# Repeating the rows of 16-wide diagonal blocks over partitions: lane shuffles on VectorE in place of selection matmuls and copies

## The chip, the cores and the metric

The kernel runs on one core of a Trainium2 chip. The metric is the device time of one execution in microseconds (us), the median over several runs. The engines are named as in the profile: PE (TensorE matmul), PEld (TensorE weight load), DVE (VectorE), ACT (ScalarE), POOL (GpSimd) and SP (SyncE). SP issues most of the loads from memory.

## The reference

The program is two layers of a hybrid backbone: 256 latent tokens and 256 context tokens of width 1024. Each layer has an input projection, three token mixers side by side (Hyena, gated DeltaNet, latent attention), a gated merge with an output projection, and a mixture of 16 experts. The second layer does not update the context. The part that matters here is the gated DeltaNet, with four heads, two directions and chunks of 64 tokens:

```python
m = jnp.where(strict, jnp.einsum('nbhid,nbhjd->nbhij', kb, kc) * gamma, 0.0)
t_inv = lax.linalg.triangular_solve(eye + m, jnp.broadcast_to(eye, m.shape), left_side=True, lower=True, unit_diagonal=True)
u = t_inv @ (vc * bc[..., None])
w = t_inv @ (kb * jnp.exp(gc)[..., None])
a_intra = jnp.einsum('nbhid,nbhjd->nbhij', qc, kc) * gamma
def step(s, xs):
    u_n, w_n, a_n, qd_n, kd_n, ge_n = xs
    v_new = u_n - w_n @ s
    o_n = qd_n @ s + a_n @ v_new
    s = s * ge_n[..., None, None] + jnp.swapaxes(kd_n, -1, -2) @ v_new
    return s, o_n
```

Every 64-wide chunk needs the inverse of a unit triangular matrix. The kernel builds it from the inverses of 16-wide diagonal blocks.

## The kernel before

The whole program is one stream of instructions per engine, and the order on each engine is fixed when the program is built. A planner keeps a virtual clock per engine (`Plan.enter`, line 254). The large projections are *items*: lists of matmuls with their weight loads and a step behind them. The mixers are *streams*, Python generators that give control back at each `yield`. After each piece of an item, `Trunk.tick` (line 490) takes the stream step that `best` (line 483) names: one whose inputs should be ready by PE's virtual clock, and only while at least 3 of the PSUM banks and some pages are free. `prep_ahead` (line 516) starts preparation of later items, and stops when VectorE's virtual clock runs far ahead of PE's. `fill` (500) and `drain` (510) run stream steps when an item must wait for data or for a stream. So the costs that `enter` charges, and the places of the `yield`s, decide which item matmuls stand on PE between the steps of a mixer.

All intermediate arrays lie in pages of 4 KB per partition, `NPAGE` of them (line 40, 45 pages), handed out by an `Arena` (line 145). Weights go to pages too, so a load waits on SP until its page is free. In the trace the page of an operand is only "pg", a PSUM bank "bank", and all instructions recorded through a helper carry line L210; so the trace is read by tiles and shapes.

The delta rule runs per layer in two streams, `gdn_pair` (line 930) for head pair 0 ("gdn0") and head pair 1 ("gdn1"). Each pair calls `gdn_system` (lines 1044 to 1200) twice, for the context tokens (base 2) and for the latent tokens (base 0), the second as a stream of its own, "gdnsys0" or "gdnsys1", started while the pair goes on. That makes 8 systems in the program. `gdn_scan` (line 1202) then runs the recurrence, the pair norms and transposes its output, and the items of the delta rule's branch come after.

One system holds 8 matrices of 128x128 (two directions, two chunk pairs, two heads). Its steps:

- E is the decay, G the key products, N the negated strict part of the system. `C` takes N's 16-wide diagonal blocks, packed as [128 partitions, 8 matrices, 16], plus the identity (lines 1084 to 1094). These are DVE operations.
- For the substitution each partition needs, of its own 16-row block, every row k. The 16 rows are repeated over their partitions: `rsel` holds 16 selection matrices of 128x128, and for each k one matmul of R[:, k, :] with the 128 elements of C (X16 from element 256) gives row k of each block on all 16 partitions (lines 1103 to 1108). Four k fill one PSUM bank, ACT copies the bank to the pages `B`, and `Bv` (line 1116) is a view of those by k. The trace shows 2 records to a matmul: 32 per system.
- The substitution (lines 1117 to 1126) goes from j = 14 down to 0 on DVE: one or two products and a reduce each, over X, P and Bv, with a `yield` after j = 10, 7, 5, 3 and 1.
- T, the inverses in block-diagonal form, is transposed on PE (weights "cst", the identity), merged from 16 to 32 to 64 by matmul groups of four 128x128 and then 64x64, with ACT and DVE operations between them that PE's next group waits for, and so is a chain over several engines.

The selection matrices come from the columns 2048 to 4095 of a constant table in memory. `late_setup` (line 2433) allocates `rsel` (8 KB per partition, 1 MB) and loads it on ACT's queue once (lines 2441 and 2442).

The items of the merge are here called gate items: of the gates of a branch, 128x512 matmuls in layer 0 and 128x256 in layer 1. `layer` (line 2293) sets their order after the mixers' items. In layer 0 a stream "filters" (started by an item hook) prepares the Hyena filters of layer 1 with 128x512 matmuls.

## Time and profile before

| | us |
|---|---|
| runs, lowest, median, highest | 2143.21, 2144.14, 2147.01 |
| the profiled execution | 2145.01 |
| its span, first to last instruction | 2143.0 |
| PE busy | 1919.7 (90%) |
| DVE busy | 1274.2 (59%) |
| ACT busy | 869.3 (41%) |
| POOL busy | 340.8 (16%) |
| mean granted TensorE clock | 0.945 |

The profiled execution is 2.0 us longer than its span and 0.87 us above the median. Busy shares are means over stages. Layer 0's mixers run from about 100 to 760 us, the experts of layer 0 to about 1200, layer 1's mixers to about 1760, its experts and the final norm to the end. In a window row the figures behind the length are the busy times of PE, PEld, DVE, ACT and POOL with the number of instructions, then the granted clock, the DMA share and the transfer rate.

### The profile page before, as it was taken

The numbers are of one execution on the slowest core, as the hardware profiler recorded it, in microseconds if no ns is written. First come the engines' busy times: TensorE is split into PE (matmuls) and PEld (weight loads), VectorE is DVE, ScalarE is ACT, GpSimd is POOL, SyncE is SP. The second block draws the span as 40 slices with busy tenths as digits, with TensorE's granted clock in tenths as the row PEclk, the third lists the DMA queues.
The fourth block names the chain that finished last, engine by engine and source line by source line (L and its number), as shares of the span: only waits on it lengthen the run. The fifth ranks groups of instructions, "written<-read, shape, count | busy, mean of one in ns | idle before, by whom it ended". The sixth has DMA issues, their size and how long they took to land. (4 is left out here: it accounts for less than half of the span.)

```text
span 2143.0 us, 31289 instructions
## 1 busy us (share of the span) xinstructions
PE 1919.7 (90%) x11901; PEld 1434.8 (67%) x11902; DVE 1274.2 (59%) x2487; ACT 869.3 (41%) x1443; POOL 340.8 (16%) x318
## 2 busy tenths in 40 slices
PE   4999999999999898799999399988999987899993
PEld 1777887877778586688777277887787976433330
DVE  3656657555466646899888676666766666311113
ACT  3442334444433323388777444433454442010101
POOL 1211122000133003411100201221011212110002
PEclk9899999999999799899999799999999998899996
DMA  9735223312533156799997567422223448899971
GB/s 330 223 96 182 60 58 94 89 50 79 158 99 85 58 180 223 256 361 382 377 358 248 173 205 234 126 55 75 79 60 109 119 138 331 294 383 389 382 269 67
DMA packets 295751, 403.62 MB, mean 188 GB/s; under 512 B 43956, under 2 KB 185786, under 8 KB 295464
## 3 DMA queue, kind: packets, MB, share of 16 engines
q1 hardware_dynamic: 271512, 360.38, 50.4%
q10 hardware_dynamic: 13040, 21.33, 2.8%
q0 software_dynamic: 11040, 19.81, 2.7%
q8 instruction: 96, 1.57, 0.3%
q14 instruction: 63, 0.52, 0.1%
HBM read 394.56 MB, written 23.20 MB: 195 GB/s over the span
## 5 line engine op out<-in xcount | busy, mean ns | idle before, releaser
L210 PE MATMUL bank<-pg,pg 128*128 128x512 f32 (+5 forms) x9958 | 1701.7, 407 | 44.3 <-DVE pg L210 23.4
L210 PEld LDWEIGHTS bank<-pg,pg 128*128 128x128 f32 (+3 forms) x9958 | 1247.5, 172 | 445.9 <-issue 204.4
L210 DVE TENSOR_TENSOR pg<-pg,pg 128x1024 fp32r<-128x1024 f32 (+10 forms) x696 | 606.1, 901 | 217.7 <-ACT pg L210 206.9
L210 ACT CAST pg<-pg 128x1024 fp32r<-128x1024 f32 (+3 forms) x460 | 428.9, 965 | 260.9 <-DVE pg L210 167.4
L210 ACT COPY pg<-bank 128x512 f32<-128x512 f32 (+4 forms) x382 | 185.0, 506 | 368.2 <-PE bank L210 335.3
L210 PE MATMUL bank<-cst,pg 128*128 128x128 f32 (+3 forms) x935 | 145.0, 292 | 90.7 <-DVE pg L210 51.9
L210 PEld LDWEIGHTS bank<-cst,pg 128*128 128x128 f32 (+1 forms) x935 | 118.8, 160 | 149.5 <-issue 54.1
L210 POOL TENSOR_TENSOR pg<-pg,pg 128x1024 f32<-128x1024 f32 (+3 forms) x77 | 133.0, 1731 | 474.8 <-DVE pg L210 243.7
L210 ACT ACTIVATE pg<-bank 128x512 f32<-128x512 f32 (+1 forms) x116 | 60.9, 534 | 201.3 <-PE bank L210 195.5
L210 POOL DMA_INDIRECT yd<-pg,t_vi x28 | 28.2, 1006 | 481.5 <-ACT pg L210 246.0
L210 DVE SCALAR_TENSOR_TENSOR pg<-pg,bank 128x512 f32<-128x512 f32 (+1 forms) x92 | 54.1, 601 | 83.1 <-ACT pg L210 72.7
L210 DVE SCALAR_TENSOR_TENSOR pg<-bank,vec,pg 128x510 f32<-128x510 f32 (+3 forms) x112 | 75.4, 676 | 44.6 <-ACT pg L210 42.6
L210 ACT ACTIVATE pg<-pg 128x512 f32<-128x512 f32 (+4 forms) x71 | 50.0, 710 | 126.9 <-DVE pg L210 101.4
L210 DVE TENSOR_TENSOR pg<-bank,pg 128x512 fp32r<-128x512 f32 (+4 forms) x120 | 69.7, 597 | 52.0 <-ACT pg L210 36.3
L210 POOL TENSOR_TENSOR pg<-pg 128x512 f32<-128x512 f32 (+1 forms) x18 | 18.5, 1032 | 440.9 <-ACT pg L210 272.7
L210 DVE COPY pg<-bank 128x512 f32<-128x512 f32 x24 | 16.6, 692 | 105.5 <-PE bank L210 92.7
L210 DVE TENSOR_TENSOR pg<-pg,bank 128x512 f32<-128x512 f32 (+1 forms) x44 | 27.0, 613 | 76.0 <-PE bank L210 74.2
L210 ACT ACTIVATE pg<-bank,vec 128x512 f32<-128x512 f32 (+3 forms) x64 | 42.1, 658 | 58.8 <-PE bank L210 53.7
L210 ACT ACTIVATE pg<-bank,t_amx,t_asq 128x512 f32<-128x512 f32 (+1 forms) x48 | 33.9, 707 | 78.8 <-DVE t_amx L210 78.8
L210 ACT CAST pg<-bank 128x512 fp32r<-128x512 f32 (+1 forms) x72 | 35.7, 520 | 73.9 <-PE bank L210 69.1
L210 PE MATMUL bank<-pg,sc 128*32 128x512 f32 x384 | 54.7, 628 | 0.9 <-DMA pg<-in_w_ada_dram 0.9
L210 DVE TENSOR_REDUCE pg<-pg 128x128 f32<-128x1024 f32 (+15 forms) x128 | 42.9, 335 | 4.4
(250 smaller groups left out, 826.9 us busy)
## 6 DMA issues: line engine op xcount, KB each, us to landing
pg<-in_moe_w_dram SPq DMA_DIRECT2D x384, 512.0 KB
pg<-in_w_in_dram SPq DMA_DIRECT2D x120, 512.0 KB
pg<-in_w_ada_dram SPq DMA_DIRECT2D x96, 512.0 KB
pg<-in_w_out_dram SPq DMA_DIRECT2D x24, 512.0 KB
pg<-modd ACTq DMA_DIRECT2D x12, 512.0 KB
pg<-yd SPq DMA_DIRECT2D x12, 512.0 KB
pg<-in_mla_w_uq_dram SPq DMA_DIRECT2D x16, 288.0 KB
pg<-gcd POOLq DMA_DIRECT2D x16, 256.0 KB, 3.9
```

Source lines behind the costliest of these rows:

```text
L210: return f(*a, **k)
```

## The change

In `gdn_system` the 16 selection matmuls and four ACT copies are gone. VectorE fills the same `B` pages from `C` by 16 `stream_shuffle`s, k from 15 down to 0. The list of 32 lanes tells each of 32 partitions from which partition of its group of 32 it reads: lane i reads 16·(i // 16) + k, which is row k of its 16-row block. Only the first k + 1 columns are copied, so the sizes fall from 8x16 to 8x1, in all 8·(16 + 15 + … + 1) = 1088 elements per partition. After k = 8 there is a new `yield`, so that the planner may put other steps there. `rsel` and its load go. `NPAGE` becomes 47: the 8 KB per partition that `rsel` held are two pages more.

```diff
@@ -37,7 +37,7 @@
 FF = 512
 CAP = (128, 96)
 BIG = 1 << 20
-NPAGE = 45
+NPAGE = 47
 def _constants():
@@ -1093,19 +1093,18 @@
         v.tensor_tensor(C, C, d16, op=OP.add)
         v.tensor_copy(X, d16)
         AT = M.get(2) if want_o else None
-        R = self.rsel
         yield
         B = [M.get(2), M.get(2)]
         if want_o:
             bQ = self.bank()
             for i, (c, h) in enumerate((c, h) for c in range(2) for h in heads):
                 t_.matmul(bQ[:, 128 * i:128 * i + 128], fm["k", h].f()[:, tok(c)], fm["q", h].f()[:, tok(c)], start=True, stop=True)
-        for q in range(4):
-            b = self.bank()
-            for k in range(4):
-                t_.matmul(b[:, 128 * k:128 * k + 128], R[:, 4 * q + k, :], X16.f(128, 256), start=True, stop=True)
-            nc.scalar.copy(B[q // 2].f(512, 512 * (q % 2)), b)
-            self.unbank(b)
+
+        Bv = [x.f().rearrange("p (k u j) -> p k u j", k=8, u=8) for x in B]
+        for k in range(15, -1, -1):
+            v.stream_shuffle(Bv[k // 8][:, k % 8, :, :k + 1], C[:, :, :k + 1], [16 * (i // 16) + k for i in range(32)])
+            if k == 8:
+                yield
         if want_o:
             mI = self.c("maskI").rearrange("p (d x) -> p d x", d=2)
             for d in range(2):
@@ -1113,7 +1112,6 @@
             self.unbank(bQ)
             g_.tensor_tensor(AT.f(), AT.f(), E.f(), op=OP.mult)
         E.free()
-        Bv = [x.f().rearrange("p (k u j) -> p k u j", k=8, u=8) for x in B]
         for j in range(14, -1, -1):
             n = 16 - j
             if j >= 8:
@@ -2438,8 +2436,6 @@
         self.rb = self.sb.tile([128, 16], F32, name="rb")
         nc.scalar.dma_start(out=self.rb, in_=a["router_b"].unsqueeze(0).to_broadcast([128, 16]))
         self.score = self.sb.tile([128, 4, 16], F32, name="score")
-        self.rsel = self.sb.tile([128, 16, 128], F32, name="rsel")
-        nc.scalar.dma_start(out=self.rsel.rearrange("p k x -> p (k x)"), in_=a["dft"][:, 2048:4096])
         self.iob, self.uSb, self.onesb = (self.tiny(128, n, BF16) for n in ("iob", "uSb", "onesb"))
         t = M.get()
         nc.scalar.dma_start(out=t.f(128), in_=a["dft"][:, 4096:4224])
```

Over the whole program DVE gets 128 shuffles (and a few rows fewer of others, as the planner's order is not the same), PE loses the 128 selection matmuls, ACT the 32 copies, and the order on PE and DVE moves at many places. Three are shown. In an order row, "pg_141_1096" is one buffer in the pages, "bank_70" a PSUM bank, "cst_72" the constants, "vec_212" a vector of weights, "x2" the number of instructions in the row.

The first place is DVE in the first system, layer 0's gdn0 on the context. Of before, pg_139_1090 is X16 and pg_155_1170 the repeated rows:

```order
L210 TENSOR_TENSOR pg_148_1143<-pg_117_794,pg_147_1142 128x1024
L210 SCALAR_TENSOR_TENSOR pg_149_1152<-bank_69,vec_212,pg_149_1152 128x2x255 x2
L210 TENSOR_TENSOR pg_153_1166<-pg_143_1112,pg_152_1165 128x1024
L210 TENSOR_TENSOR pg_141_1096<-bank_70,cst_72 128x512 x2
L210 TENSOR_TENSOR pg_139_1090<-pg_139_1090,pg_155_1170 128x8x2
L210 TENSOR_REDUCE pg_139_1090<-pg_139_1090 128x8
L210 TENSOR_TENSOR pg_139_1090<-pg_139_1090,pg_155_1170 128x8x3
L210 TENSOR_REDUCE pg_139_1090<-pg_139_1090 128x8
```

Of the change, pg_141_1092 is X16, and pg_157_1172 and pg_156_1171 the two page pairs of the repeated rows:

```order
L210 TENSOR_TENSOR pg_155_1168<-pg_138_1048,pg_154_1167 128x1024
L210 STREAM_SHUFFLE pg_157_1172<-pg_141_1092 128x128
L210 STREAM_SHUFFLE pg_157_1172<-pg_141_1092 128x8x15
L210 STREAM_SHUFFLE pg_157_1172<-pg_141_1092 128x8x14
L210 STREAM_SHUFFLE pg_157_1172<-pg_141_1092 128x8x13
L210 STREAM_SHUFFLE pg_157_1172<-pg_141_1092 128x8x12
L210 STREAM_SHUFFLE pg_157_1172<-pg_141_1092 128x8x11
L210 STREAM_SHUFFLE pg_157_1172<-pg_141_1092 128x8x10
L210 STREAM_SHUFFLE pg_157_1172<-pg_141_1092 128x8x9
L210 TENSOR_TENSOR pg_159_1213<-bank_65,pg_159_1213 128x2x128 x2
L210 SCALAR_TENSOR_TENSOR pg_160_1224<-bank_67,vec_216,pg_160_1224 128x2x255 x2
L210 STREAM_SHUFFLE pg_156_1171<-pg_141_1092 128x8x8
```

Before, the substitution begins directly behind the two operations on bank_70 (AT). Now eight shuffles stand first, two steps of other mixers follow at the new `yield`, and then the other eight shuffles.

The second place is PE at the end of layer 0, in the last system of that layer (gdnsys1). Rows of four 128x128 are the merge from 16 to 32 to 64, rows of 64x64 the last merge, and the 128x512 rows into bank_68 are a gate item:

```order
L210 MATMUL bank_67<-pg_474_5086,pg_469_4877 128x128 x4
L210 MATMUL bank_63<-pg_469_4877,pg_474_5086 128x128 x4
L210 MATMUL bank_68<-pg_77_400,pg_481_5114 128x512 x2
L210 MATMUL bank_68<-pg_77_400,pg_482_5115 128x512
L210 MATMUL bank_68<-pg_78_409,pg_481_5114 128x512 x2
L210 MATMUL bank_68<-pg_78_409,pg_482_5115 128x512
L210 MATMUL bank_66<-pg_380_3771,pg_466_4846 64x64 x4
L210 MATMUL bank_66<-pg_472_5079,pg_466_4846 64x64 x4
L210 MATMUL bank_68<-pg_80_419,pg_481_5114 128x512 x2
L210 MATMUL bank_68<-pg_80_419,pg_482_5115 128x512
```

Of the change, with the gate item's rows into bank_70:

```order
L210 MATMUL bank_70<-pg_83_432,pg_474_4766 128x512 x2
L210 MATMUL bank_70<-pg_83_432,pg_475_4767 128x512
L210 MATMUL bank_68<-pg_494_5101,t_fw_99 64x256
L210 MATMUL bank_65<-cst_71,pg_505_5181 128x128 x4
L210 MATMUL bank_64<-cst_71,pg_505_5181 128x128 x4
L210 MATMUL bank_66<-pg_502_5173,t_fw_100 64x256
L210 MATMUL bank_69<-pg_506_5182,pg_483_4943 128x128 x4
L210 MATMUL bank_67<-pg_506_5182,pg_483_4943 128x128 x4
L210 MATMUL bank_63<-pg_495_5102,pg_502_5173 128x512
L210 MATMUL bank_70<-pg_495_5102,pg_502_5173 128x512
L210 MATMUL bank_68<-pg_507_5185,pg_505_5181 128x128 x4
L210 MATMUL bank_65<-pg_505_5181,pg_507_5185 128x128 x4
```

Before, the gate item stands between the groups of the merge. Now the last gate item ends ahead of the transposes of T (weights cst_71), and the groups follow each other with only the rows of the filter stream (t_fw) between. Of 48 matmuls of gate items that stood behind those transposes before, none does now. A block of 48 filter matmuls of 128x512, which stood behind the whole of this pair before, now stands behind the second merge, at the rows after the ones shown.

The third place is PE at the end of layer 1, in that layer's last system:

```order
L210 MATMUL bank_69<-pg_1676_12971,pg_1727_13568 64x64 x4
L210 MATMUL bank_69<-pg_1744_13899,pg_1727_13568 64x64 x4
L210 MATMUL bank_68<-pg_1385_9806,pg_1751_13941 128x256 x2
L210 MATMUL bank_68<-pg_1385_9806,pg_1752_13942 128x256
L210 MATMUL bank_68<-pg_1388_9822,pg_1751_13941 128x256 x2
L210 MATMUL bank_68<-pg_1388_9822,pg_1752_13942 128x256
L210 MATMUL bank_68<-pg_1389_9831,pg_1751_13941 128x256 x2
L210 MATMUL bank_68<-pg_1389_9831,pg_1752_13942 128x256
L210 MATMUL bank_68<-pg_1390_9840,pg_1751_13941 128x256 x2
L210 MATMUL bank_68<-pg_1390_9840,pg_1752_13942 128x256
L210 MATMUL bank_70<-pg_1699_13233,pg_1504_10896 64x64 x4
```

Of the change:

```order
L210 MATMUL bank_68<-pg_1403_9869,pg_1760_13909 128x256 x2
L210 MATMUL bank_68<-pg_1403_9869,pg_1761_13910 128x256
L210 MATMUL bank_64<-cst_71,pg_1411_9913 128x128 x4
L210 MATMUL bank_65<-cst_71,pg_1686_12958 128x128 x4
L210 MATMUL bank_70<-pg_1774_14019,pg_1748_13674 128x128 x4
L210 MATMUL bank_67<-pg_1774_14019,pg_1748_13674 128x128 x4
L210 MATMUL bank_69<-pg_1775_14022,pg_1411_9913 128x128 x4
L210 MATMUL bank_66<-pg_1411_9913,pg_1775_14022 128x128 x4
L210 MATMUL bank_63<-pg_1775_14022,pg_1686_12958 128x128 x4
L210 MATMUL bank_68<-pg_1686_12958,pg_1775_14022 128x128 x4
L210 MATMUL bank_64<-pg_1774_14019,pg_1748_13674 128x128 x4
```

The 128x256 rows into bank_68 are gate items here. Before, they stand between the 64x64 groups of the last merge; now they end ahead of the transposes, and the merge runs group on group. Of 72 matmuls of gate items that stood behind the transposes before, none does now.

## Rows read from the trace of the kernel before

**Rows 1.** The page, part 1: busy time of each engine, share of the span, instructions.

```profile
PE 1919.7 (90%) x11901; PEld 1434.8 (67%) x11902; DVE 1274.2 (59%) x2487; ACT 869.3 (41%) x1443; POOL 340.8 (16%) x318
```

**Rows 2.** Windows by stage: stretch, its length, busy us (instructions) by engine, PEclk, DMA, GB/s.

```profile
100.00:700.00 600.00, 590.66 (x3375) 472.32 (x3374) 363.07 (x795) 244.58 (x463) 95.78 (x98) 0.99 0.34 97
...
700.00:760.00 60.00, 49.80 (x191) 35.05 (x190) 36.97 (x80) 18.20 (x30) 4.07 (x4) 0.77 0.24 74
...
1250.00:1720.00 470.00, 430.93 (x3041) 376.24 (x3041) 312.12 (x729) 201.71 (x395) 66.65 (x75) 0.95 0.37 107
```

**Rows 3.** Waits of PE, 100 to 740 us: on whom, total us, times, longest.

```profile
PE bank L210 <- ACT pg L210: 9.5, 9, 2.3
...
PE bank L210 <- DVE pg L210: 4.7, 9, 1.3
```

**Rows 4.** Waits of PE, 1235 to 1760 us, the same columns.

```profile
PE bank L210 <- DVE pg L210: 21.5, 19, 4.6
...
PE bank L210 <- POOL pg L210: 15.8, 6, 8.0
...
PE bank L210 <- ACT pg L210: 15.1, 13, 3.1
```

**Rows 5.** Lines by form, whole span: shape xcount | busy, mean ns | idle.

```profile
L210 PE MATMUL bank<-pg,rsel 128*128 128x128 f32 x256 | 34.8, 302 | 4.6 <-DVE pg L210 4.6
...
L210 ACT COPY pg<-bank 128x512 f32<-128x512 f32 x220 | 126.5, 587 | 299.5 <-PE bank L210 282.2 <-issue 8.0 <-DMA pg<-in_moe_w_dram 5.1
```

**Rows 6.** Timeline of the first system: start us, us, engine, line, operation, count, idle before.

```profile
156.26 1.16 PE L210 MATMUL bank<-pg,pg 128*128 128x128 f32 x8
...
157.26 3.74 PE L210 MATMUL bank<-pg,rsel 128*128 128x128 f32 x32
...
161.03 0.59 ACT L210 COPY pg<-bank 128x512 f32<-128x512 f32 x1 [0.31 <-PE bank L210]
...
161.65 0.94 DVE L210 TENSOR_TENSOR pg<-pg,pg 128x16 f32<-128x16 f32 x1 [1.60 <-ACT pg L210]
```

**Rows 7.** Lines by form, 100 to 700 us: the small VectorE operations.

```profile
L210 DVE TENSOR_REDUCE pg<-pg 128x8 f32<-128x16 f32 x4 | 0.7, 172 | 0.1
...
L210 DVE TENSOR_REDUCE pg<-pg 128x8 f32<-128x128 f32 x4 | 1.2, 289 | 0.1
...
L210 DVE COPY pg<-cst 128x128 f32<-128x128 f32 x4 | 0.9, 220 | 0.0
```

**Rows 8.** Timeline of VectorE at the end of layer 1: a smallest operation, 128x4.

```profile
1744.11 0.16 DVE L210 TENSOR_TENSOR t_oss<-t_oss,t_osc 128x4 f32<-128x4 f32 x1
```

**Rows 9.** Windows around two of the eight systems, columns as in rows 2.

```profile
148.00:180.00 32.00, 29.95 (x202) 22.54 (x195) 26.11 (x55) 9.84 (x16) 4.38 (x3) 1.00 0.49 149
...
592.00:625.00 33.00, 32.14 (x188) 24.46 (x185) 29.07 (x54) 10.51 (x16) 16.01 (x13) 1.00 0.48 144
```

**Rows 10.** Timeline of PE, end of layer 0's mixers.

```profile
585.61 5.79 PE L210 MATMUL bank<-pg,pg 128*128 128x512 f32 x24
...
655.60 3.74 PE L210 MATMUL bank<-pg,rsel 128*128 128x128 f32 x32
...
675.62 1.04 PE L210 MATMUL bank<-cst,pg 128*128 128x128 f32 x8
...
726.01 0.69 PE L210 MATMUL bank<-cst,pg 128*128 128x128 f32 x2 [4.61 <-POOL pg L210]
```

**Rows 11.** Timeline of PE, end of layer 1's mixers.

```profile
1698.71 7.24 PE L210 MATMUL bank<-pg,pg 128*128 128x256 f32 x46 [2.13 <-DVE pg L210]
...
1706.10 1.26 PE L210 MATMUL bank<-cst,pg 128*128 128x128 f32 x8
...
1748.11 1.11 PE L210 MATMUL bank<-cst,pg 128*128 128x128 f32 x4 [8.04 <-POOL pg L210]
```

**Rows 12.** Waits of the SP queue, whole span: on whom, total us, times, longest.

```profile
SPq L210 <- DVE pg L210: 610.8, 126, 57.2
```

**Rows 13.** Windows, 80 to 100 us, columns as in rows 2.

```profile
80.00:100.00 20.00, 16.11 (x64) 12.89 (x64) 10.84 (x33) 7.32 (x12) 5.28 (x9) 0.83 0.69 225
```


## The prediction

> **What bounds the kernel now.** I read the busy line of the page first: PE works 90% of the span, VectorE 59%, ScalarE 41% [rows 1]. A share over the whole span hides its stages, so the windows come next [rows 2]. From 100 to 700 us, layer 0's mixers, PE is busy 590.66 of 600 us: almost every microsecond taken off PE there comes off the end, as long as something else stands ready. VectorE is busy 363.07 us there. At the end of those mixers, 700 to 760 us, PE works 49.80 of 60. In layer 1's mixers, 1250 to 1720 us, it is 430.93 of 470. The list of PE's waits names who it waits for: in layer 0 ScalarE with 9.5 us and VectorE with 4.7 [rows 3]; in layer 1 VectorE with 21.5 us over 19 waits and POOL with 15.8 over 6, the longest 8.0 [rows 4]. So PE binds, and the two mixer tails, where a short chain over all engines runs without enough other work on PE, are where it stands still.
>
> **The selection matmuls.** The forms show 256 of them, 34.8 us of PE in all, and the copies of 128x512 at 587 ns each [rows 5]. The timeline of the first system shows 32 records in 3.74 us [rows 6]; eight systems make 8 × 3.74 = 29.9 us, the other 5 us lie in systems where the records are longer. The same timeline gives the time this step takes on the chain of its own system: from the first selection matmul at 157.26 to the substitution's first product at 161.65 are 4.4 us, and the last copy stands directly ahead of it (161.03 + 0.59 = 161.62). The matmuls stand in PE's order, so all other work on PE waits 3.74 us too. The four copies are 4 × 0.59 = 2.4 us of ScalarE per system, 19 us in all. ScalarE is not the bound; I count them at nothing, and the work on PE covers them.
>
> **The shuffles.** The trace of before has none. The nearest rows are small VectorE operations on 128 partitions: a reduce over 128x16 takes 172 ns, one over 128x128 takes 289 ns, the copy of 128x128 220 ns [rows 7], and an operation of 128x4, as small as any, 160 ns [rows 8]. From the two reduces, one element more costs (289 − 172) / 112 = 1.04 ns, and nothing at all costs about 155 ns. The 16 shuffles of a system have 1088 elements: 16 × 0.155 + 1088 × 0.00104 = 3.6 us. Below that, if they run like the copy (220 − 155 = 65 ns for 128 elements): 16 × 0.155 + 1088 × 0.0005 = 3.0 us; I round the lower end to 2.7 us, 22 us for eight systems. Above, if each needs a second instruction for its list of lanes, at the floor of 160 ns: 3.6 + 16 × 0.16 = 6.2 us, 50 us in all. I take the middle, 4.9 us per system and 39 us in all, since the list must get to the engine somehow, and an operation without data may be shorter than the floor. So on the chain of one system 4.4 us go and 4.9 come, about nothing. The new step doesn't wait for PE or ScalarE, but stands in VectorE's order, and what stands behind it there waits up to 4.9 us longer.
>
> [...]
>
> **Who waits for VectorE then.** Around a system of layer 0, VectorE is already busy 26.11 of 32 us and 29.07 of 33 us [rows 9]. With 4.9 more it is 31.0 of 32 and 34 of 33. What is queued behind are items' preparations and the products of the other streams, whose results PE takes next. Over the whole stage, 363.07 of 600 us, it has room [rows 2], so the excess of a microsecond or two moves on into the next stretch and only a part becomes waits of PE.
>
> **The order.** The planner charges other costs, so its streams run further behind the items. In layer 0 a system of the second pair has 58 more item matmuls ahead of it, in layer 1 the second pair starts behind 80 more. At the end of both layers this takes the cover away, as the second and third place of the order show: the items that stood between the last system's transposes of T and the end of its pair (layer 0: 48 matmuls; layer 1: 72) now stand ahead of these transposes. In before an item of 24 matmuls of 128x512 takes 5.79 us, so 48 take 11.6 us [rows 10]. In layer 1, 46 matmuls of 128x256 take 7.24 us, 0.157 each beside other work [rows 11]; by the size it is half of 5.79 / 24 = 0.24 us, 0.12, which I take: 72 × 0.12 = 8.6 us.
> - *Layer 0.* The chain runs from the transposes at 675.62 to the output's transposes at 726.01, which wait 4.61 us for POOL [rows 10]. Without cover, PE waits on this chain up to 11.6 us more. Against that, the block of 48 filter matmuls of 128x512 (11.6 us at most) moves into it, but in one piece, which fills only the one wait it stands in. I take two thirds of 11.6, 7.7 us, nearer to the end of the waits that [rows 10] shows, since PE stood still here even with its cover. Three of the four systems of this layer lie where PE is full and give 3 × 3.74 = 11.2 us; the fourth is in the tail and gives nothing (4.4 against 4.9). Sum: −11.2 + 7.7 = −3.5 us, ends −12 (the block covers all) and +5 (all the cover is lost, and VectorE's 4.9 us come on top).
> - *Layer 1.* The same: −11.2 us from three systems, two thirds of 8.6, 5.8 us, back in the tail between 1706.10 and 1748.11, where the last step already waits 8.04 us for POOL [rows 11]. Sum: −5.4 us, ends −15 and +5.
>
> **Pages and the load.** SP waits 610.8 us in all for pages that VectorE holds [rows 12], so two more pages let loads start earlier; PE's waits in both mixers name no transfer [rows 3, 4], so this gives nothing there: 0, ends −3 and 0. The load of 1 MB stood at 89 us, where the DMA engines work at 0.69 of their time [rows 13] and no wait of PE names it: 0. The page that is held longer by a late system could stall a load; I count 0.
>
> **Sum.** −3.5 − 5.4 = −9 us against the profiled execution's 2145.0: 2136. The profiled execution lies 0.87 us above the median, so against the median it is 2135. A measurement of this kernel can tell about 0.2%, 4.3 us.
>
> **Rivals.**
> - *Full gain.* The lost cover costs nothing, since PE's queue behind the chain is never empty, and all of PE's selection work comes off: −34.8 us, 2110 us (2109 against the median). For it: PE at 590.66 of 600 us. Against it: PE waited already in the tails, and 9 of the 35 us lie in the two last systems. Chance 0.23.
> - *VectorE binds.* If the lists of lanes cost the full 6.2 us or more, then in each of the six full systems VectorE saturates the windows above: what comes off PE, 3.74 us, is given back as waits for VectorE, and the tails lose a bit: 2145 ± 3, no change. For it: 29.07 of 33 us, and VectorE as first of the releasers in layer 1. [...] Chance 0.17.
> - *Slower: the last systems run bare.* Its place is the two tails. There the whole chain of a system, its merge, the scan and the norm runs without items between. If PE waits for all of the lost cover, that is 11.6 + 8.6 = 20 us. At 6.2 us of shuffles against 4.4 the two tails grow by 1.8 us each, 4 us, and the full windows overflow (26.11 + 6.2 is 0.3 us over 32, 29.07 + 6.2 is 2.3 over 33), 1.3 us on average for each of six systems, 8 us. Against that stand 6 × 3.74 = 22.4 us: +9 us, 2154 (2153 against the median), with 2150 to 2156 about it. It decides from the point where the shuffles cost over about 6.2 us per system, or the filter block's 11.6 us stand in front of a step that the chain needs. For it: waits of 4.61 and 8.04 us in just these places. Against it: a block of other work still stands in layer 0's chain. Chance 0.18.
>
> That the shuffles don't take the place of the matmuls is excluded: the matmul rows are gone from PE's order.
>
> **How the numbers follow.** The forecast, −9 us with ends of about −16 and −2, has 0.42. The full gain lies at 2110, so the range reaches down to 2108; upward it takes the no-change case and most of the slower one, to 2153. Faster by over 0.2% (below 2140): nearly all of the forecast and the full gain, 0.39 + 0.23 = 0.62. Within 0.2%: most of the VectorE case and the forecast's upper edge, 0.14 + 0.03 = 0.17. Slower: the last rival and the rest of the VectorE case, 0.18 + 0.03 = 0.21.
>
> **What would show it.** Right: PE busy falls by about 35 us and VectorE's rises by 30 to 45; shuffles of 0.16 to 0.3 us each; in the six full systems PE stays without a gap; in the windows after the transposes of T in both layers, PE's idle time grows by 5 to 8 us. Wrong: shuffles over 0.4 us each, or PE waiting for VectorE inside the six systems (then the VectorE rival), or tails as short as before (then the full gain), or tails longer by 15 us or more each (then the slower one).

## The result and the profile after

The change is slower: 2165.9 us (median of 4 runs) against 2143.68 us, ratio 1.0101 with a 95% interval of 1.0085 to 1.0116, some 22 us. That is outside the range of 2108 to 2153 us. The profiled execution has a span of 2164.0 us where before had 2143.0.

The busy line of the page after, to set beside [rows 1]:

```profile
PE 1888.1 (87%) x11645; PEld 1408.8 (65%) x11646; DVE 1299.7 (60%) x2743; ACT 852.2 (39%) x1411; POOL 341.7 (16%) x318
```

PE lost 31.6 us of work, near the forecast, and VectorE gained 25.5 us. With 31.6 us less work and a span 21.0 us longer, PE stands idle 52.6 us more. The lines by form give the price of the new operations (count | busy, mean ns | idle):

```profile
L210 DVE STREAM_SHUFFLE pg<-pg 128x128 f32<-128x128 f32 x8 | 2.4, 296 | 0.0
...
L210 DVE LOAD_MASK_SELECT pg<-pg x128 | 1.8, 14 | 0.0
...
L210 DVE STREAM_SHUFFLE pg<-pg 128x8 f32<-128x8 f32 x8 | 1.6, 196 | 0.0
```

Ahead of every shuffle the trace shows one more operation, LOAD_MASK_SELECT, which I take for the load of its list of lanes: 128 of them for 128 shuffles, 14 ns each. So the shuffles are cheap, and still the kernel is slower.

**By stage.** Three marks are the same in every version: the first matmul of the routing in each layer, and the long wait between the layers. Of before, in PE's timeline (start, us, engine, line, operation, idle before):

```profile
878.18 0.20 PE L210 MATMUL bank<-t_rA,t_uSb 128*128 128x48 bf16 x1 [9.06 <-DVE t_rA L210]
...
1230.96 1.05 PE L210 MATMUL bank<-cst,pg 128*128 128x128 f32 x3 [33.28 <-DVE pg L210]
...
1816.85 0.17 PE L210 MATMUL bank<-t_rA,t_uSb 128*128 128x16 bf16 x1 [10.16 <-DVE t_rA L210]
```

Of the change:

```profile
899.73 0.20 PE L210 MATMUL bank<-t_rA,t_uSb 128*128 128x48 bf16 x1 [8.93 <-DVE t_rA L210]
...
1248.07 1.04 PE L210 MATMUL bank<-cst,pg 128*128 128x128 f32 x3 [33.15 <-DVE pg L210]
...
1837.57 0.17 PE L210 MATMUL bank<-t_rA,t_uSb 128*128 128x16 bf16 x1 [10.80 <-DVE t_rA L210]
```

Layer 0's mixers take 21.6 us more, layer 0's experts 4.4 less (348.3 for 352.8), layer 1's mixers 3.6 more (589.5 for 585.9), the rest 0.3 more. Most of the loss lies in layer 0's mixers. That layer's windows, of before and then of the change (columns as in [rows 2]):

```profile
100.00:600.00 500.00, 493.55 (x2728) 391.26 (x2727) 303.72 (x655) 205.92 (x395) 63.36 (x63) 0.99 0.34 98
600.00:878.20 278.20, 248.48 (x1297) 199.20 (x1296) 169.01 (x341) 94.12 (x152) 71.38 (x56) 0.92 0.45 149
```

```profile
100.00:600.00 500.00, 477.58 (x2594) 376.43 (x2594) 303.79 (x712) 197.19 (x379) 59.48 (x55) 0.98 0.33 94
600.00:899.70 299.70, 249.70 (x1301) 203.59 (x1300) 180.12 (x411) 93.37 (x150) 74.57 (x58) 0.91 0.43 145
```

PE's idle time grows from 6.5 to 22.4 us in the first stretch and from 29.7 to 50.0 us in the second: 36 us, of which 15 are work removed and 21 are lost.

**Two places.** The first system, in the timeline of the change beside [rows 6]:

```profile
158.61 0.30 DVE L210 STREAM_SHUFFLE pg<-pg 128x128 f32<-128x128 f32 x1
...
159.93 0.28 DVE L210 STREAM_SHUFFLE pg<-pg 128x72 f32<-128x72 f32 x1
...
163.47 0.42 DVE L210 TENSOR_TENSOR pg<-bank,pg 128x256 fp32r<-128x256 f32 x1 [3.25 <-ACT pg L210]
...
166.73 0.22 DVE L210 STREAM_SHUFFLE pg<-pg 128x64 f32<-128x64 f32 x1
...
168.84 0.18 DVE L210 TENSOR_TENSOR pg<-pg,pg 128x16 f32<-128x16 f32 x1
...
178.33 1.88 PE L210 MATMUL bank<-cst,pg 128*128 128x8 f32 x8 [8.85 <-ACT pg L210]
```

The first half of the shuffles ends at 160.2. Then come the steps that the planner put at the new `yield`; they wait 3.25 us for ScalarE, and since VectorE follows its order, the other half waits with them until 166.73. The substitution begins at 168.84, where before it began at 161.65 [rows 6]. What is queued behind is late as well, and PE stands still for 8.85 us.

The end of both layers' mixers, in PE's timeline of the change beside [rows 10, 11]:

```profile
692.66 0.61 PE L210 MATMUL bank<-pg,t_fw 33*64 33x256 f32 x2 [3.61 <-DMA pg<-in_dft_dram]
...
702.68 1.97 PE L210 MATMUL bank<-cst,pg 128*128 128x128 f32 x8 [9.41 <-DVE pg L210]
...
765.66 0.69 PE L210 MATMUL bank<-cst,pg 128*128 128x128 f32 x2 [9.05 <-POOL pg L210]
```

```profile
1733.78 1.97 PE L210 MATMUL bank<-cst,pg 128*128 128x128 f32 x8 [11.09 <-DVE pg L210]
...
1770.52 1.12 PE L210 MATMUL bank<-cst,pg 128*128 128x128 f32 x4 [7.99 <-POOL pg L210]
```

The transposes of T, ahead of which no item work was left, wait 9.41 and 11.09 us for the substitution, and the output's transposes in layer 0 wait 9.05 us where they waited 4.61.

### The profile page after: what moved, and what is told of

Same layout as the page of the kernel before. It is cut to its first block, busy times and chain, and to the rows that moved or that the text cites. A ratio compares the mean times of both kernels' runs of the same rounds, so it can differ in the third digit from the quotient of the medians.

```text
span 2164.0 us, 30985 instructions
## 1 busy us (share of the span) xinstructions
PE 1888.1 (87%) x11645; PEld 1408.8 (65%) x11646; DVE 1299.7 (60%) x2743; ACT 852.2 (39%) x1411; POOL 341.7 (16%) x318
## 5 line engine op out<-in xcount | busy, mean ns | idle before, releaser
L210 PE MATMUL bank<-pg,pg 128*128 128x512 f32 (+6 forms) x9976 | 1702.5, 407 | 56.6 <-ACT pg L210 36.9
L210 PEld LDWEIGHTS bank<-pg,pg 128*128 128x128 f32 (+4 forms) x9976 | 1256.1, 173 | 452.7 <-issue 204.5
L210 DVE TENSOR_TENSOR pg<-pg,pg 128x1024 fp32r<-128x1024 f32 (+12 forms) x692 | 610.8, 912 | 218.1 <-ACT pg L210 208.9
L210 ACT COPY pg<-bank 128x512 f32<-128x512 f32 (+3 forms) x350 | 166.7, 499 | 393.4 <-PE bank L210 357.4
L210 POOL TENSOR_TENSOR pg<-pg,pg 128x512 f32<-128x512 f32 (+3 forms) x76 | 131.8, 1740 | 442.0 <-DVE pg L210 226.2
```

The costliest lines, as they stand in the source:

```text
L210: return f(*a, **k)
```

## The experiments

Sixteen kernels ran. Where a kernel keeps another's order, the planner is charged as that one's was and the instructions are put in past it; only the instructions named then differ on any engine. Times are medians, each beside runs of before on the same chip; ratios are to those.

**1. The change in parts, and a cross of order and method.** e1 drops the new yield; e2 keeps it and has 45 pages:

```diff
-            if k == 8:
-                yield
```

```diff
-NPAGE = 47
+NPAGE = 45
```

e3 is before with the method alone changed:

```diff
-                t_.matmul(b[:, 128 * k:128 * k + 128], R[:, 4 * q + k, :], X16.f(128, 256), start=True, stop=True)
-            nc.scalar.copy(B[q // 2].f(512, 512 * (q % 2)), b)
+                self.plan.enter("tensor", "matmul", ...)
+            self.plan.enter("scalar", "copy", ...)
...
+        for k in range(15, -1, -1):
+            nc._nc.vector.stream_shuffle(Bs[k // 8][:, k % 8, :, :k + 1], C[:, :, :k + 1], ...)
```

and e4 is e2 with the method alone changed back:

```diff
-            v.stream_shuffle(Bv[k // 8][:, k % 8, :, :k + 1], C[:, :, :k + 1], ...)
+            self.plan.enter("vector", "stream_shuffle", ...)
+            if k % 8 == 0:
+                for q in ((2, 3) if k else (0, 1)):
...
+                        raw.tensor.matmul(b[:, 128 * i:128 * i + 128], self.rsel[:, 4 * q + i, :], X16.f(128, 256), ...)
+                    raw.scalar.copy(B[q // 2].f(512, 512 * (q % 2)), b)
...
```

Expected of e1: 

> The change without its new yield after k = 8; the 16 shuffles then stand together on VectorE. Theory A (the order: the planner's new places for items and stream steps cost the 22 us, the shuffles themselves are cheap): the order still differs from before's at many places, so the time lies anywhere between 2130 and 2166 us. Rival B (the yield: two steps of other streams that wait for PE stand between the halves of the shuffles and hold VectorE, 3.25 us idle in the first system): 2130 to 2145 us, and no wait of 8 us of PE in the first system. Rival C (VectorE binds: any 16 shuffles per system cost the gain): 2160 to 2170 us. Rival D (two pages more spoil the order): 2160 us or more.

Of e2: 

> The change with 45 pages, as before, and the new yield. Theory A: the order changes again against the change (some 800 of 9373 matmuls move) and stays far from before's; 2145 to 2175 us. Rival B (the yield): as the change, 2160 to 2170 us. Rival C (VectorE binds): 2160 to 2170 us. Rival D (the two pages): 2125 to 2145 us.

Of e3: 

> Before with shuffles in place of the matmuls and copies, while the planner is charged as if these were still there: on PE, VectorE and ScalarE all other instructions stand exactly as before, 45 pages, no new yield, the load of the selection matrices kept. Theory A: the shuffles by themselves gain, since 16 of them take 2.5 us where the old chain took 4.4, and 30 us of PE work go: 2110 to 2135 us. Rival B (the yield): the same, 2110 to 2140. Rival C (VectorE binds): 2155 to 2170 us, as the change. Rival D: about 2120 to 2144.

Of e4: 

> The 45-page version of the change with the selection matmuls and copies put back at the places of the two halves of the shuffles, while the planner is charged as if they were shuffles: everything else stands in the order of e2_45_pages. Theory A: slower than e2_45_pages, by up to the 30 us of PE work: 2170 to 2195 us, far over before, with the same work in it. Rival B (the yield): also slow, 2165 to 2190. Rival C (VectorE binds): faster than e2_45_pages, 2135 to 2150 us, as before.

| | us | ratio to before | 95% interval |
|---|---|---|---|
| e1, 47 pages, no yield | 2153.35 | 1.0041 | 1.0027 to 1.0055 |
| e2, 45 pages, yield | 2184.47 | 1.0185 | 1.0168 to 1.0202 |
| e3, shuffles in before's order | 2152.84 | 1.0048 | 1.0031 to 1.0064 |
| e4, matmuls in e2's order | 2194.28 | 1.0248 | 1.0217 to 1.0279 |

No theory had all four, and B, C and D had no range right. e3 refutes A's gain: with not one other instruction moved, the shuffles cost 0.48%, some 10 us, though PE has 30 us less to do. e4 refutes C's other half: the same work as before's, in e2's order, is 2.5% slower. So there are two costs, one of the method and one of the order. The method's sign hangs on the order: it costs 0.5% in before's and gains some 0.6% in e2's. e1 and e3 run the same shuffles, e3 in before's order and e1 in one of its own, and take the same time: e1's order shows no cost beyond e3's. From e1 to the change it is 0.6% more, some 13 us, and that comes with the yield and the places that move with it. In e1 the wait of 8.85 us in the first system is gone; its first wait of PE above 3 us after 100 us comes at 289. e2 and e4, which have the yield, show it again, with 8.84 and 6.20 us.

**2. What the method costs in before's order.** e3's timeline shows the place. First before, in a system of layer 0, VectorE and what it holds up:

```profile
592.50 4.15 DVE L210 TENSOR_TENSOR pg<-pg,pg 128x1024 fp32r<-128x1024 f32 x2
...
596.58 1.27 DVE L210 TENSOR_TENSOR pg<-bank,cst 128x512 f32<-128x512 f32 x2
...
597.77 0.17 DVE L210 TENSOR_TENSOR pg<-pg,pg 128x16 f32<-128x16 f32 x1
...
616.48 0.66 PE L210 MATMUL bank<-cst,pg 128*128 128x128 f32 x4 [0.50 <-DVE pg L210]
```

and e3:

```profile
597.30 0.29 DVE L1111 STREAM_SHUFFLE pg<-pg 128x128 f32<-128x128 f32 x1
...
599.69 1.28 DVE L210 TENSOR_TENSOR pg<-bank,cst 128x512 f32<-128x512 f32 x2
...
600.90 0.17 DVE L210 TENSOR_TENSOR pg<-pg,pg 128x16 f32<-128x16 f32 x1
...
619.48 2.13 PE L210 MATMUL bank<-cst,pg 128*128 128x128 f32 x8 [5.58 <-DVE pg L210]
```

In before the matmuls and copies ran (593.33 to 597.69) while VectorE worked through other operations; it reached the substitution at 597.77 without a gap. In this system the selection cost VectorE's line nothing. The shuffles stand in that line: 597.30 to 599.69 is 2.4 us. PE, relieved of 3.74 us, comes earlier to the transposes and waits 5.58 us there, for 0.50 before.

This is the only one of the eight systems in which VectorE did not wait for ScalarE's last copy. The substitution's small products over the whole span (count | busy, mean ns | idle before), first of before, then of e3:

```profile
L210 DVE TENSOR_TENSOR pg<-pg,pg 128x24 f32<-128x24 f32 x16 | 6.3, 395 | 0.5
...
L210 DVE TENSOR_TENSOR pg<-pg,pg 128x16 f32<-128x16 f32 x16 | 5.1, 317 | 15.2 <-ACT pg L210 15.1
```

```profile
L210 DVE TENSOR_TENSOR pg<-pg,pg 128x24 f32<-128x24 f32 x16 | 16.5, 1033 | 0.5
...
L210 DVE TENSOR_TENSOR pg<-pg,pg 128x16 f32<-128x16 f32 x16 | 2.9, 179 | 0.1
```

In before VectorE waited 15.1 us for the copies in the other seven systems, and in e3 not at all. In five of these waits, wholly or in part, POOL worked on its product of AT and E, which six systems have. In the kernel before, in the second system:

```profile
243.67 2.36 POOL L210 TENSOR_TENSOR pg<-pg,pg 128x1024 f32<-128x1024 f32 x1 [19.49 <-PE bank L210]
...
247.88 0.19 DVE L210 TENSOR_TENSOR pg<-pg,pg 128x16 f32<-128x16 f32 x1 [4.43 <-ACT pg L210]
```

In e3 the substitution begins beside POOL's product in all six, and there its product of 128x24 takes 2.2 to 2.3 us in place of 0.2 (part 3). In before one took 2.36 us so, and two of 128x16 took 0.94 and 1.47. The two rows together grow from 11.4 to 19.4 us. So on VectorE's line 15 us of waits go, 19 us of shuffles (8 × 2.4) come, and 8 us of products that POOL holds up: some 12 us more, where the kernel is some 10 us slower.

Two kernels part the two halves of the swap, both in before's order. e5 adds the shuffles and keeps the matmuls; e6 drops the matmuls and adds no shuffle, so that the blocks are not repeated:

```diff
+        for k in range(15, -1, -1):
+            nc._nc.vector.stream_shuffle(P[:, :, :k + 1], C[:, :, :k + 1], ...)
```

```diff
-                t_.matmul(b[:, 128 * k:128 * k + 128], R[:, 4 * q + k, :], X16.f(128, 256), start=True, stop=True)
-            nc.scalar.copy(B[q // 2].f(512, 512 * (q % 2)), b)
...
+            nc._nc.scalar.copy(B[q // 2].f(512, 512 * (q % 2)).rearrange(...), C[:, None, :, :].to_broadcast([128, 4, 8, 16]))
```

> Before, with its matmuls and copies, and beside them the 16 shuffles per system, written to a place that the substitution overwrites: all in before's order, so only VectorE gets 8 x 2.4 = 19 us more. Theory E (VectorE's queue around each system is what ends last; it is followed in order and has no gap there): 10 to 19 us slower than before, 2154 to 2164 us. Rival F (PE bounds and VectorE has room, the shuffles hurt only where they replace cover): 0 to 4 us slower, 2144 to 2149.

> Before without the selection matmuls and without shuffles: ScalarE's four copies read C directly, so the blocks aren't repeated (the rows of the substitution are wrong in value); all else in before's order. PE loses 30 us of work, VectorE gains none. Theory E: the 30 us come back mostly as PE's waits for VectorE, 2 to 12 us faster than before, 2133 to 2143. Rival F: 20 to 30 us faster, 2115 to 2125 us.

Measured: e5 2159.62 us, 1.0079 (1.0048 to 1.0109), some 17 us slower; e6 2135.76 us, 0.9967 (0.9954 to 0.9980), 7 us faster. Both lie in theory E's ranges, but e5 with another load than E took. Its 16 shuffles all write one place, and each starts only after the one ahead has ended:

```profile
598.95 0.29 DVE L1110 STREAM_SHUFFLE pg<-pg 128x128 f32<-128x128 f32 x1
...
599.28 0.30 DVE L1110 STREAM_SHUFFLE pg<-pg 128x120 f32<-128x120 f32 x1
...
603.32 1.28 DVE L210 TENSOR_TENSOR pg<-bank,cst 128x512 f32<-128x512 f32 x2
```

So they take 4.4 us per system, 35 us in all and not 19. Of these 35 us on VectorE's line 17 come on (with the interval, 10 to 23); of 30 us of PE work 7 come off. That the two add up to +0.46%, near e3's +0.48%, is then chance in part. e6's timeline shows a part of where PE's time went, in the same system:

```profile
614.02 2.13 PE L210 MATMUL bank<-cst,pg 128*128 128x128 f32 x8 [3.20 <-DVE pg L210]
```

The other part is PE's own pace. The busy lines of e3 and of e6, to set beside [rows 1]:

```profile
PE 1901.4 (89%) x11645; PEld 1411.5 (66%) x11646; DVE 1301.0 (61%) x2743; ACT 852.1 (40%) x1411; POOL 341.9 (16%) x318
```

```profile
PE 1905.9 (89%) x11645; PEld 1413.6 (66%) x11646; DVE 1283.4 (60%) x2487; ACT 868.2 (41%) x1443; POOL 341.5 (16%) x318
```

Matmuls of 34.8 us [rows 5] are gone, but PE's busy time is only 18.3 us lower in e3 and 13.8 in e6: the matmuls that stay took some 15 and 20 us longer, while PE's idle time grew by 24 and 13 us. The mean granted clock was 0.938 and 0.935, in before 0.945; in the window of [rows 9] it was 0.90 in both, where before had 1.00:

```profile
592.00:625.00 33.00, 26.91 (x131) 17.83 (x131) 30.28 (x86) 8.68 (x11) 15.40 (x13) 0.90 0.47 144
```

```profile
592.00:625.00 33.00, 29.69 (x144) 21.18 (x145) 26.30 (x53) 8.34 (x12) 13.76 (x12) 0.90 0.44 137
```

The trace of e6 is of an execution of 2143.87 us; its other seven took 2131.5 to 2138.26 us at clocks of 0.939 to 0.943, so there the share of the pace is smaller. Theory E, which knew only waits, is thus half of the account.

**3. POOL's product moved to VectorE.** The same stretch of before shows what POOL's product of AT and E costs VectorE:

```profile
598.07 2.41 POOL L210 TENSOR_TENSOR pg<-pg,pg 128x1024 f32<-128x1024 f32 x1 [2.50 <-ACT pg L210]
598.19 2.36 DVE L210 TENSOR_TENSOR pg<-pg,pg 128x24 f32<-128x24 f32 x1
```

VectorE's product of 128x24 takes as long as POOL's of 128x1024. In the kernel before it does so in this system alone, in e3 and in the change in all six that have POOL's product. e8 (in e3), e9 (in before) and e12 (in the change) put this product on VectorE, with the order kept:

```diff
-            g_.tensor_tensor(AT.f(), AT.f(), E.f(), op=OP.mult)
+            self.plan.enter("gpsimd", "tensor_tensor", (AT.f(), AT.f(), E.f()), {})
+            nc._nc.vector.tensor_tensor(AT.f(), AT.f(), E.f(), op=OP.mult)
```

> e3_old_order (shuffles in before's order) with the product of AT and E taken from POOL to VectorE, in the six systems that have it, the planner charged as if on POOL. In the trace a product of 128x24 on VectorE takes 2.3 us while POOL works on this one, 0.2 us otherwise, so VectorE loses some 2.1 us to it and would spend about 1.2 us on it itself. Theory E (VectorE's queue counts): 3 to 7 us faster than e3_old_order, 2146 to 2150 us. Rival F: the same time or a little slower, 2152 to 2157.

> Before, with its selection matmuls, and only the product of AT and E taken from POOL to VectorE in the six systems that have it; the planner is charged as if on POOL, so all else stands as before. Theory E (VectorE's queue counts, e8 against e3 gave 10.8 us): 6 to 12 us faster than before, 2131 to 2138 us, which would beat both kernels. Rival F: the same time, 2141 to 2147.

> The change as it is, with the product of AT and E taken from POOL to VectorE in six systems, all else in the change's own order. Theory E: 6 to 11 us faster than the change, 2155 to 2160 us, in this order as in before's. Rival F: as the change, 2163 to 2168 us.

In e8 the pair of rows reads

```profile
599.51 1.23 DVE L1118 TENSOR_TENSOR pg<-pg,pg 128x1024 f32<-128x1024 f32 x1
...
601.08 0.20 DVE L210 TENSOR_TENSOR pg<-pg,pg 128x24 f32<-128x24 f32 x1
```

so VectorE spends 1.23 us more on the one and over 2 us less on the other. Measured: e8 2142.01 us, 0.9996 (0.9983 to 1.0009), where e3 had 1.0048, more than E expected; e9 2141.64 us, 0.9984 (0.9971 to 0.9997), and e12 2165.09 us, 1.0105 (1.0083 to 1.0126), both in rival F's ranges. E took e3's relief for e9's, but before has one such product where e3 has six: by the busy lines VectorE's work falls by 4.5 us from e3 to e8 and by 7.4 from the change to e12, and rises by 2.5 from before to e9. e9's gain of 0.16% is hardly clear of zero.

With the product on VectorE in both, shuffles (e8) and matmuls (e9) differ in before's order by 0.12%, within the intervals. So most of the method's 0.48% in that order goes when POOL's product goes: the shuffles cost little by their own length, and more by bringing the substitution beside POOL. In the change's order the same relief of VectorE gave nothing; what ends last there these runs don't show.

**4. What an order costs.** e7 has neither the yield nor the two pages. e10 starts the second head pair earlier in e1, so that the tails are covered:

```diff
-QPOS = (4, 2)
+QPOS = (3, 1)
```

e11 and e15 (in before) and e16 (in e1) change one number of the planner, 100 to 50, 150 and 200; e13 (in e1) and e14 (in before) charge VectorE's operations more:

```diff
-        self.slack, self.backlog = 100.0, 4000.0
+        self.slack, self.backlog = 50.0, 4000.0
```

```diff
-                c = 70 + (0.52 if fast else 1.04) * n + ...
+                c = 190 + (0.52 if fast else 1.04) * n + ...
```

> The change without the new yield and with 45 pages. Theory G (the new yield costs some 13 us by itself, as e1_no_yield against the change): 10 to 18 us faster than e2_45_pages, 2166 to 2175 us. Rival H (each new order is a throw of its own, and neither yield nor pages has a sign): anywhere from 2135 to 2190, and no sum of the two single differences (which would give 2172).

> e1_no_yield (shuffles, 47 pages, no new yield) with the second head pair started earlier in both layers (QPOS 3 and 1 where it was 4 and 2), so that in layer 0 108 and in layer 1 228 item matmuls stand behind the last transposes of T in place of 52 and 0. Theory G (the bare tails cost 15 to 20 us of the change): 8 to 20 us faster than e1_no_yield, 2133 to 2145 us. Rival H (each order is a throw; covering the tails moves the waits to another place): 2148 to 2175 us.

> Before with one number of the planner changed that means nothing to the work: a stream step may be late by 50 ns of PE's virtual clock, where it was 100. 705 of 9501 matmuls change places, no instruction is added or taken. Theory H (each order is a throw): 2150 to 2185 us, like the other orders. Rival G (only orders that bare the tails are slow; this one has 52 and 48 item matmuls there): 2140 to 2152 us.

> e1_no_yield (shuffles, 47 pages, no new yield) with the planner's fixed charge of a VectorE operation raised from 70 to 190 ns, near what the small operations of the substitution take in the trace (0.21 us from one to the next at 128x16). Some thousand matmuls change places. Theory I (the new orders are slow because the planner charges the VectorE chain too little): 8 us or more faster than e1_no_yield, under 2146 us. Rival H (each order is a throw): anywhere from 2140 to 2185.

> Before with the same charge of 190 ns in the planner, nothing else: no instruction is added or taken. Theory I: as fast as before or faster, 2125 to 2147 us. Rival H: before's order is a good throw and each other one costs, 2152 to 2185.

> Before with a stream step allowed to be late by 150 ns of PE's virtual clock (100 in before, 50 in e11_slack): 399 of 9501 matmuls change places. Rival H: 2150 to 2185 us again. Theory G (only bare tails cost; here the last tail has 96 item matmuls, more than before's 72): 2138 to 2148.

> e1_no_yield with 200 ns in the same place: 231 of 9373 matmuls change places, the last tail of layer 1 stays without item matmuls. Rival H: off e1_no_yield by 5 us or more, to either side. Theory G: as e1_no_yield, 2149 to 2157 us, since the tails are the same.

| | us | ratio to before | 95% interval |
|---|---|---|---|
| e7, 45 pages, no yield | 2178.39 | 1.0163 | 1.0141 to 1.0185 |
| e10, tails covered | 2174.67 | 1.0152 | 1.0129 to 1.0175 |
| e11, before, slack 50 | 2167.56 | 1.0115 | 1.0090 to 1.0139 |
| e15, before, slack 150 | 2156.07 | 1.0064 | 1.0040 to 1.0087 |
| e16, e1 with slack 200 | 2165.15 | 1.0108 | 1.0083 to 1.0132 |
| e13, e1 with charge 190 | 2224.9 | 1.0384 | 1.0355 to 1.0413 |
| e14, before with charge 190 | 2233.03 | 1.0421 | 1.0397 to 1.0445 |

e11 and e15 are the plainest: the same instructions as before, in other places (705 and 399 of 9501 matmuls, as counted ahead of the runs), and 1.15% and 0.64% slower. e16 moves 231 matmuls against e1, with the same bare tail in layer 1, and loses 0.67% against e1. Theory G falls: e7 gains 6 us on e2 and not 10 to 18, covering the tails (e10) was slower than leaving them bare (e1), and orders with covered tails are slow too. Theory I falls: the truer charge makes both methods 3 to 4% slower. Theory H had e7, e10, e11, e15 and e16 in its ranges, which are wide, and missed e13 and e14, which came out 40 and 48 us above them. As far as these runs go, before's order is better than nine of the ten others tried, the change's counted: with matmuls e4, e11, e14 and e15 came out 0.6% to 4.2% slower than before, with shuffles the change, e2, e7, e10, e13 and e16 0.5% to 3.3% slower than e3. e1's order, with two pages more and without the load of the selection matrices, does as well as before's with the same shuffles, so not every new order costs. In e11 the waits look like those of the change, with the matmuls kept:

```profile
693.40 1.97 PE L210 MATMUL bank<-cst,pg 128*128 128x128 f32 x8 [4.72 <-DVE pg L210]
...
755.08 0.69 PE L210 MATMUL bank<-cst,pg 128*128 128x128 f32 x2 [9.14 <-POOL pg L210]
```

## Why the prediction was wrong

The change's 22 us are some 10 us of the method, as e3 measures it in an order that stays, and some 13 us that come with the new yield and the order that it brings (e1 against the change); one changed number of the planner (e11) costs as much as both. They don't simply add, since the method's sign changes with the order (e4 against e2).

- **The matmuls go: right in size, wrong in worth.** In the change PE's busy time fell by 31.6 us, near the 34.8 forecast. The step that failed is "three of the four systems lie where PE is full and give 3 × 3.74 = 11.2 us" per layer. e6 shows that taking all of it away gives 7 us in the whole program. I took PE, with its 4.7 us of waits for VectorE [rows 3], as the one bound, and VectorE's 363.07 of 600 us [rows 2] as room. The waits were small in part because the selection matmuls stood where PE would have waited: with them gone PE stood still 13 us more in e6 and 24 in e3, and its other matmuls took some 20 and 15 us longer at a lower granted clock (a mean of 0.935 and 0.938, in before 0.945). The sum had no term for either. Around a system both engines were near their limit (29.07 of 33 us [rows 9]): VectorE's additions show (e5), and PE's relief hardly does (e6).
- **The shuffles: too dear in the forecast.** I took 4.9 us per system, with 2.7 as the lower end; they take 2.4. The load of a list of lanes costs 14 ns where I allowed up to 160, and one shuffle starts 0.21 us after the other at 128 elements though each lasts 0.30. In e5, where each starts only after the one ahead has ended, they take 4.4 us, so it is the overlap that I left out. By its record a shuffle of 128x128 takes 296 ns in the change, about as long as the addition of the identity to C at the same size, 293 ns.
- **"On the chain of one system 4.4 us go and 4.9 come, about nothing": wrong.** The 4.4 us ran for the greater part beside other work of VectorE. What counts is what stands on the line that is followed in order. There the old step took 15.1 us of waits in seven of the eight systems, 1.60 of them in the first [rows 6]; the new one takes 19 us, and 8 us more of products that POOL holds up. POOL I put at nothing without a reason, though [rows 6] shows a product of 128x16 at 0.94 us, where an operation of 128x4 takes 0.16 [rows 8]. e8 shows the worth of it: without POOL's product most of the method's loss is gone.
- **The tails: seen, too small, and not the cause by themselves.** In layer 0 PE's idle time after 600 us grew by 20 us where I gave back 7.7; in layer 1 the mixers as a whole lost 3.6 us where I forecast a gain of 5.4. The waits of 9.41 and 11.09 us stand where the second and third place of the order had no item left. But e10, which covers them, is slower.
- **The yield: not forecast.** I described its place and gave it no price. Its wait in the first system is shown by the kernels with and without it. Without it the change takes 2153.35 us, 13 us less; that the yield alone is worth 13 us is not shown, as it also changes the order, and the same step at 45 pages gives 6 us, within the intervals of e2 and e7.
- **The pages: 0 was wrong.** From 45 to 47 pages the change gains about 18 us with the yield (2184.47 to 2165.9) and 25 without. I can't part fewer waits for pages from yet another order.
- **The rivals.** "VectorE binds" had the right engine and the wrong point: I let it decide from 6.2 us per system, and 2.4 us with POOL's product behind them were enough. The slower rival had its place in the tails and its limit at 2156. What both lacked was the price of a new order itself.
- **The ends.** The forecast's ends of about −16 and −2 don't follow from the two layers' own, which add up to −27 and +10. The measured 22 us lie outside both.

What stays open is why before's order is better than most: these runs show that it is, not which of its many places make it so. Open is also why the shuffles gain in e2's order.

## What to carry to other kernels

Where two engines are both nearly full around a step, work taken off one and put on the other must be priced on the line of the one that receives it, in its order, and the waits of the giver are no measure of the receiver's room. Look too at what a third engine did in the waits that go: here POOL's product had run in them, and then ran against the work that came. Where a planner sets the order, test a change once with the order held as it was, and once with only the order disturbed: here a number without meaning cost as much as the whole change. A place where other streams may step in, between two halves of something that an in-order engine has ready, makes the second half wait for them: VectorE stood still 3.25 us there in the first system.

## What the runs showed of the hardware

- In e3 a shuffle over 128 partitions takes 0.19 to 0.32 us by its record and starts 0.09 to 0.21 us after the one ahead; in e5, where all write one place, 0.22 to 0.34 us after it. The LOAD_MASK_SELECT ahead of each takes 14 ns in the change, 128 times in the program.
- While POOL multiplied 128x1024 elements (2.41 us), VectorE's product of 128x24 took 2.36 us; with POOL's product gone it took 0.20 (e8). So here POOL's product held one of VectorE for nearly its whole length; in e3 it does so in six systems, where VectorE's product takes 2.2 to 2.3 us.
- Behind one wait PE itself was slower. After the 5.58 us in e3 the eight transposes and the eight matmuls of the next item took 2.13 and 1.63 us; in before four of the transposes took 0.66 us (616.48) and the item's eight 1.07. First e3, its window from 616 to 622 us and the item's row, then before's row:

```profile
616.00:622.00 6.00, 2.52 (x12) 1.63 (x16) 5.91 (x7) 0.89 (x2) 4.91 (x5) 0.50 0.51 143
```

```profile
621.53 1.63 PE L210 MATMUL bank<-pg,sc 128*32 128x512 f32 x8
```

```profile
618.08 1.07 PE L210 MATMUL bank<-pg,sc 128*32 128x512 f32 x8
```

  The granted clock in e3's window, which begins within the wait (it ended at 619.48), is 0.50; before's over the same stretch is 1.00. From the first transpose to the end of the item's eight it is 3.68 us in e3 and 2.67 in before, so this wait cost about one microsecond more than its length.
